# Output projection: the last twelve column tiles computed as six Strassen pairs

## The chip, the cores and the metric

The kernel runs on one core of a Trainium2 chip. Its engines are TensorE (PE in the profile; its weight loads are listed apart as PEld), VectorE (DVE), ScalarE (ACT), GpSimd (POOL) and SyncE (SP, which here only issues DMAs). They run side by side, each through its own list of instructions in a fixed order, and wait for each other through semaphores. The metric is the device time of one execution in microseconds; times below are medians of several executions.

## The reference, cut to what matters

One layer of a decoder: a combined input projection, two token mixers (sparse attention and a gated linear recurrence), a merge, and an output projection with a residual. 512 prompt tokens and 64 sample tokens share the weights, so the kernel treats them as 576 columns. The change touches only the last line:

```
u_att = einsum('btc,cd->btd', o_att * silu(g_att), w_att_out)
u_rnn = einsum('btc,cd->btd', h_rnn * silu(g_rnn), w_rnn_out)
m = sigmoid(gm_att) * u_att + sigmoid(gm_rnn) * u_rnn
return x + einsum('btd,de->bte', m, w_out)        # 576 x 2048 times 2048 x 2048
```

## The kernel before

Everything is kept with channels on the 128 partitions and the 576 tokens along the free dimension, cut into two halves h of 288 columns. A projection's output is cut into tiles of 128 channels. The list `tiles` holds them in order of work: input projection, then `ur` and `ua` (the two branch projections, whose merged result is the activation m, in 16 row blocks of 128 channels), then `y`, the 16 tiles of the output projection. Each `y` tile has two units u: a unit is 8 weight blocks of 128x128, one half of the 2048 rows that are summed.

A **slot** is the work of one unit on one half: 24 matmuls of 288 columns (L1483 to L1485). There are three for each weight block because float32 is kept by splitting both operands into a high part and a rest: high weight times high activation, high times rest, rest times high. A `y` tile has four slots (h0u0, h0u1, h1u0, h1u1), and its two units are added up in one PSUM bank for each half. The banks have tags: `g`, `s` and `t` with two each, `o` and `m` with one.

Weights come in by DMA (`raw`, two buffers). ACT rounds a unit to its high part (`w_high`, tile `whi`, L210), and DVE subtracts to get the rest (`w_low`, tile `wlo`, L216). Both have three buffers in rotation (`WHL = 3`), so the split of a unit waits until the matmuls of the unit three before have read theirs. After a half of a `y` tile is summed, DVE evacuates the bank and adds the residual (L541), and SP stores the tile (L543).

What sets the order: the program is written out slot by slot, and each engine gets its instructions in the order in which the code emits them. In each turn of the slot loop that is: the high parts that are due, then what was booked for this slot with `at(...)`, then the low parts and the next weight loads, the residual loads, then the evacuations (`evac`) of the products that the turn before emitted, then what was booked "behind", and last this slot's own matmuls. So on DVE a turn's low part stands ahead of its evacuations. The unit `(n, u, at)` in `wunits` says in which turn a unit is split.

Of the kernel before, what the change touches and what calls it, by code (L numbers as in the profile page):

```python
# [10 lines left out]
F = mybir.dt.float32  # L11
R = mybir.dt.float32r
# [12 lines left out]
FULL = (0, 1)  # L25
CF, PG = 18, 22
SCH = 22, 38, 66, 5

D = 2048
SEQ = 512  # L30
DB = 8
# [82 lines left out]
def nsa_rglru_step(ctx, tc, a, o):  # L114
# [25 lines left out]

    cst = cp.tile([128, CONST.shape[1]], F, name="cst")
    par = cp.tile([128, NPAR], F, name="par")
    wcs = cp.tile([128, 4, 32], F, name="wcs")
    wcp = cp.tile([128, 32], F, name="wcp")
    pt_sb = cp.tile([1, DB * NPAGE], I32, name="pt_sb")

# [12 lines left out]
    ot_d = {g: dp.tile([128, 2, 512], F, name=f"ot_{g}") for g in range(KG)}  # L159
    kc_d = {b: dp.tile([128, 4, 64], F, name=f"kc_{b}") for b in range(KEPT, DB)}  # L160
    gs_d = dp.tile([48, 64], F, name="gs_d")

# [15 lines left out]
    slots, wunits = [], []  # L178
# [19 lines left out]
    def w_load(k):  # L198
        if k >= len(wunits):
            return  # L200
        n, u, _ = wunits[k]
        t = wp.tile([128, 8, 128], F, tag="raw", name="raw", bufs=WRAW)
        S.dma_start(t, tiles[n][2][u])
        raw[k] = t
# [90 lines left out]
    rstd = cp.tile([128, NT], F, name="rstd")  # L295
    e2 = cp.tile([128, NT], F, name="e2")
    e2t = cp.tile([128, 4], F, name="e2t")
    gq8 = cp.tile([128, 1], F, name="gq8")
# [45 lines left out]
    def etile(name):  # L344
        return ep.tile([128, NT], F, tag="e", name=name, bufs=4)

# [6 lines left out]
    def evac(kind, h, b):  # L353
        hs = slice(h * HF, h * HF + HF)
        z = b[:, :HF]
        name = kind[0]
        if name == "gn":
            if h == 0:
# [166 lines left out]
        elif name == "ua":  # L525
# [7 lines left out]
            A.activation(mh[j][:, hs], m[:, hs], AF.Copy)  # L533
            V.tensor_sub(ml[j][:, hs], m[:, hs], mh[j][:, hs].bitcast(F))
        elif name == "y":
            j = kind[1]
            if h == 0:
                held["y"] = etile("y")
            t = held["y"]
            r = res_in[j]  # L540
            V.scalar_tensor_tensor(t[:, hs], z, 0.25, r[:, hs], OP.mult, OP.add)  # L541
            if h == 1:
                store(lambda: S.dma_start(o["y"][j], t), 1)  # L543
# [778 lines left out]


    psteps, ssteps, pages = prompt_steps(), None, compress()
    prompt_done = False
# [33 lines left out]
    def first_products(s):  # L1359
# [13 lines left out]
        if s == 7:  # L1373
            for h in range(2):
                evs.append((tiles[1][0], h, gbs[h]))

    def sample_work(s):
# [8 lines left out]
    for s, (n, h, u) in enumerate(slots):  # L1386
        now[0] = s
        kind, m, units = tiles[n]
        if s == slot_of[first_r]:
# [7 lines left out]
            att.close()  # L1397
            rp_["h"] = ctx.enter_context(tc.tile_pool(name="hp", bufs=1))
            rp_["s"] = ExitStack()
            rp_["p"] = rp_["s"].enter_context(tc.tile_pool(name="rp", bufs=1))  # L1400
            rnn_begin()
        if s == slot_of[first_u] - 9:
# [3 lines left out]
            rp_["s"].close()  # L1406
            rp_["p"] = ctx.enter_context(tc.tile_pool(name="up", bufs=1))
            for ct in range(8):
                at(s + 3 * ct // 2, lambda ct=ct: oa_make(ct))
        ws = []  # L1410
        while wnext < len(wunits) and wunits[wnext][2] <= s:
# [33 lines left out]
        for n2 in range(n, len(tiles)):  # L1445
# [6 lines left out]
            if name == "y" and j not in res_in:  # L1452
                res_in[j] = rp_["p"].tile([128, NT], F, tag="tgi", name="res", bufs=4)
                S.dma_start(res_in[j], xin[j // 2, :, j % 2, :])
        for e in evs:
# [5 lines left out]
        if n == 1:  # L1461
            first_products(s)
            continue
        wh, wl = whl[n, u]
        last = u == len(units) - 1
        for step, (h2, k) in enumerate([(h, k) for k in range(8)]):
# [12 lines left out]
            elif name == "y":  # L1479
                r_h, r_l = mh[kk], ml[kk]  # L1480
            else:
                r_h, r_l = xh[kk], xl[kk]
# [19 lines left out]
def _layout(x):  # L1502
# [83 lines left out]
```

## Time and profile before

| | us |
|---|---|
| median of 3 runs (1724.31 to 1725.62) | 1725.07 |
| the profiled execution | 1724.24 |
| its span | 1722.5 |
| PE busy / DVE busy / ACT busy | 1691.8 / 1074.8 / 796.8 |
| granted TensorE clock, mean | 0.999 |
| `y` stage, from about | 1515 |
| last matmul starts | 1718.61 |

The page counts an engine's busy time, cuts the span into slices, follows the chain of work that ended last back from the end, and groups instructions by line. The line numbers are those of the kernel before. Matmuls are pipelined: one is listed as 0.29 us long, but the next starts some 0.13 us after it.

### The profile page before, as it was taken

The numbers are of one execution on the slowest core, as the hardware profiler recorded it, in microseconds if no ns is written. First come the engines' busy times: TensorE is split into PE (matmuls) and PEld (weight loads), VectorE is DVE, ScalarE is ACT, GpSimd is POOL, SyncE is SP. The second block draws the span as 40 slices with busy tenths as digits, with TensorE's granted clock in tenths as the row PEclk, the third lists the DMA queues.
The fourth block names the chain that finished last, engine by engine and source line by source line (L and its number), as shares of the span: only waits on it lengthen the run. The fifth ranks groups of instructions, "written<-read, shape, count | busy, mean of one in ns | idle before, by whom it ended". The sixth has DMA issues, their size and how long they took to land. (4 is left out here: it accounts for less than half of the span.)

```text
span 1722.5 us, 33473 instructions
## 1 busy us (share of the span) xinstructions
PE 1691.8 (98%) x12637; PEld 1661.5 (96%) x12637; DVE 1074.8 (62%) x2290; ACT 796.8 (46%) x1487; POOL 476.9 (28%) x503
## 2 busy tenths in 40 slices
PE   9999999999999999999999999999999999999999
PEld 8999989998998999999999999999999999999999
DVE  6578678778867876457777775676664344432221
ACT  6434553553455454367677663666663122211110
POOL 0035334442543344165555540000013111100000
PEclk9999999999999999999999999999999999999999
DMA  6367435434533444367576664222226434333432
GB/s 221 119 208 236 153 105 167 123 111 128 156 117 110 146 143 140 120 183 211 186 215 202 188 187 127 79 92 78 92 95 234 134 115 135 127 127 126 143 115 78
DMA packets 143139, 248.55 MB, mean 144 GB/s; under 512 B 19457, under 2 KB 78466, under 8 KB 142722
## 3 DMA queue, kind: packets, MB, share of 16 engines
q1 hardware_dynamic: 142978, 246.42, 44.5%
q8 instruction: 99, 1.62, 0.4%
q14 instruction: 62, 0.51, 0.1%
HBM read 223.40 MB, written 31.35 MB: 148 GB/s over the span
## 5 line engine op out<-in xcount | busy, mean ns | idle before, releaser
L1483 PE MATMUL g<-xh,whi 128*128 128x288 f32 x2400 | 717.1, 299 | 0.1
L1485 PE MATMUL g<-xh,wlo 128*128 128x288 f32 x2400 | 708.3, 295 | 2.8 <-DVE wlo L216 2.7
L1484 PE MATMUL g<-xl,whi 128*128 128x288 f32 x2400 | 707.4, 295 | 0.0
L1485 PEld LDWEIGHTS g<-xh,wlo 128*128 128x128 f32 x2400 | 450.8, 188 | 3.7 <-DVE wlo L216 3.7
L1483 PEld LDWEIGHTS g<-xh,whi 128*128 128x128 f32 x2400 | 451.4, 188 | 1.6 <-ACT c L388 0.3
L1484 PEld LDWEIGHTS g<-xl,whi 128*128 128x128 f32 x2400 | 451.3, 188 | 1.3
L216 DVE TENSOR_TENSOR wlo<-raw,whi 128x1024 fp32r<-128x1024 f32 x216 | 282.9, 1310 | 105.8 <-ACT whi L210 105.5
L210 ACT ACTIVATE whi<-raw 128x1024 fp32r<-128x1024 f32 x216 | 227.4, 1053 | 214.9 <-PE g L1484 209.8
L835 POOL TENSOR_TENSOR cr<-cr,wcs 128x512 f32<-128x512 f32 x128 | 179.6, 1409 | 143.8 <-DMA cr<-in_cmp 126.2
L1485 PE MATMUL g<-mh,wlo 128*128 128x288 f32 x512 | 150.8, 295 | 0.0
L1484 PE MATMUL g<-ml,whi 128*128 128x288 f32 x512 | 150.8, 294 | 0.0
L687 ACT ACTIVATE p<-p,sm,rq 128x128 f32<-128x128 f32 (+3 forms) x128 | 83.0, 650 | 146.4 <-DVE sm L684 146.4
L1483 PE MATMUL g<-mh,whi 128*128 128x288 f32 x512 | 150.7, 294 | 0.0
L944 POOL TENSOR_TENSOR skl<-kr,skh 128x512 fp32r<-128x512 f32 x80 | 114.2, 1430 | 122.5 <-ACT skh L943 88.1
L695 POOL TENSOR_SCALAR p<-p,sm 128x128 f32<-128x128 f32 (+3 forms) x128 | 70.3, 562 | 220.5 <-DVE sm L692 98.5
L706 DVE TENSOR_TENSOR pt<-t,pt 128x512 fp32r<-128x512 f32 x96 | 66.2, 689 | 64.3 <-ACT pt L705 62.9
L1485 PEld LDWEIGHTS g<-mh,wlo 128*128 128x128 f32 x512 | 96.0, 188 | 0.0
L1483 PEld LDWEIGHTS g<-mh,whi 128*128 128x128 f32 x512 | 96.0, 188 | 0.0
L1484 PEld LDWEIGHTS g<-ml,whi 128*128 128x128 f32 x512 | 96.0, 188 | 0.0
L1046 DVE TENSOR_TENSOR sv<-vr,sv 128x256 fp32r<-128x256 f32 (+1 forms) x120 | 77.4, 672 | 17.5 <-ACT sv L1042 17.3
L841 DVE TENSOR_REDUCE skvx<-cr 128x16 f32<-128x512 f32 x128 | 86.6, 677 | 0.4
L533 ACT ACTIVATE mh<-ur 128x288 fp32r<-128x288 f32 x32 | 14.3, 447 | 145.0 <-POOL ur L529 145.0
(323 smaller groups left out, 2985.8 us busy)
## 6 DMA issues: line engine op xcount, KB each, us to landing
raw<-in_w_in SPq DMA_DIRECT2D x152, 512.0 KB, 3.5
cr<-in_cmp SPq DMA_DIRECT2D x128, 256.0 KB, 3.6
kr<-in_selk SPq DMA_DIRECT2D x128, 128.0 KB, 3.1
vr<-in_selv SPq DMA_DIRECT2D x128, 128.0 KB, 3.1
raw<-in_w_out SPq DMA_DIRECT2D x32, 512.0 KB, 3.3
tg<-gm SPq DMA_DIRECT2D x32, 288.0 KB, 4.4
tgi<-tg SPq DMA_DIRECT2D x32, 288.0 KB, 3.9
raw<-in_w_rnn SPq DMA_DIRECT2D x16, 512.0 KB, 3.5
```

Of the source, the lines that this page charges most:

```text
L210: A.activation(hi, raw[k], AF.Copy)
L216: V.tensor_sub(lo, raw.pop(k), hi.bitcast(F))
L687: A.activation(p[:, :n], p[:, :n], AF.Exp, bias=sm[:, 1, r - r0:r - r0 + 1], scale=rq[:, i, r:r + 1], accum_out=sm[:, 2, r - r0:r - r0 + 1])
L695: G.tensor_scalar(p[:, :n], p[:, :n], sm[:, 3, r - r0:r - r0 + 1], 1.0, op0=OP.mult, op1=OP.mult)
L706: V.tensor_sub(lo, t, hi.bitcast(F))
L835: G.tensor_tensor(v, v, wcs[:, :, None, :].to_broadcast([128, 4, 4, 32]), op=OP.mult)
L841: V.tensor_reduce(x.kvx[:, :, 8 + n * 4:12 + n * 4], v, axis=AX.X, op=OP.add)
L944: G.tensor_tensor(kl, t, kh.bitcast(F), op=OP.subtract)
L1046: V.tensor_sub(v[:, :, :, 1, :], src, v[:, :, :, 0, :].bitcast(F))
L1483: T.matmul(gb[:, :HF], wh[:, k, :], r_h[:, hs], start=kk == 0, stop=False)
L1484: T.matmul(gb[:, :HF], wh[:, k, :], r_l[:, hs], start=False, stop=False)
L1485: T.matmul(gb[:, :HF], wl[:, k, :], r_h[:, hs], start=False, stop=last and k == 7)
```

## The change

The tiles `y` 0 to 3 stay as they were (`YSTD = 4`), but for which row blocks make up a unit: u0 now has the even blocks of m, u1 the odd ones. The tiles 4 to 15 are taken two at a time (j, j+1) as kind `Y`, and a pair is computed with Strassen's scheme in Winograd's form: the output is seen as 2x2 (two channel tiles, two token halves), the sum over rows as two halves (even, odd blocks). Seven products of one slot each take the place of eight. Four sums of weight units (`y_sum`, DVE) and four sums of activations for each pair of row blocks (`y_factors`, DVE) feed them. The activation sums are made once, in the slots of the first four tiles, from float32 rows of m that are stored to HBM when they are made (`m_d`) and read back (`y_fetch`). A product is added from PSUM into one, two or three quarters of the residual tile (`y_evac`), and two pairs of products share a bank: u2 is summed on top of u0, u6 on top of u3. The unit of a product is split three turns ahead of its slot.

Beside this, `e` tiles have five buffers instead of four, some constants move to a pool that is closed early, and the weight rows lie in another order in HBM.

```diff
-    for j in range(16):
+    for j in range(YSTD):
         tiles.append((("y", j), 128, [a["w_out"][j, 0], a["w_out"][j, 1]]))
+    for j in range(YSTD, 16, 2):
+        tiles.append((("Y", j), 128, [None] * 7))
...
+        if kind[0] == "Y":
+            for u in range(7):
+                slots.append((n, 0, u))
+                unit_of[n, u] = len(wunits)
+                wunits.append((n, u, base - 3 + u))
+            continue
...
+            if h == 1:
+                S.dma_start(m_d[j], m)
             A.activation(mh[j][:, hs], m[:, hs], AF.Copy)
             V.tensor_sub(ml[j][:, hs], m[:, hs], mh[j][:, hs].bitcast(F))
...
+    def y_factors(i):
+        e, f = e12.pop(i)
+        lo_, hi_ = slice(0, HF), slice(HF, NT)
+        V.tensor_sub(e[:, lo_], e[:, hi_], e[:, lo_])
+        V.tensor_sub(e[:, hi_], f[:, hi_], e[:, hi_])
+        V.tensor_sub(f[:, hi_], f[:, hi_], e[:, lo_])
+        V.tensor_sub(f[:, lo_], f[:, lo_], f[:, hi_])
+        for t, pool, tag, to in ((e, "h", "hr", t13), (f, "p", "t42", t42)):
...
+            A.activation(hi, t, AF.Copy)
+            V.tensor_sub(lo, t, hi.bitcast(F))
...
+        if which == 1:
+            t = ysum[1] = wp.tile([128, 8, 128], F, tag="raw", name="s1", bufs=WRAW)
+            V.tensor_add(t, a21, yraw[j, 1, 1])
+            units = {0: a11, 2: yraw[j, 0, 1], 5: t, 6: yraw[j, 1, 1]}
+        elif which == 2:
+            t = ysum[2] = wp.tile([128, 8, 128], F, tag="raw", name="s2", bufs=WRAW)
+            V.tensor_sub(t, ysum[1], a11)
+            units = {4: t}
+        elif which == 3:
+            V.tensor_sub(a21, a11, a21)
+            units = {3: a21}
+        else:
+            V.tensor_sub(a11, yraw[j, 0, 1], ysum[2])
+            units = {1: a11}
...
+    def y_plan(n, j):
+        b = slot_of[n]
+        at(b - 7, lambda: y_load(j, 0, 0))
+        at(b - 6, lambda: (y_load(j, 0, 1), y_load(j, 1, 1)))
+        at(b - 6, lambda: y_load(j, 1, 0), True)
+        for which, s in ((1, b - 5), (2, b - 4), (3, b - 3), (4, b - 3)):
+            at(s, lambda which=which: y_sum(n, j, which), True)
...
+    YPROD = ((0, 0, "g", True), (1, 1, "s", True), (1, 0, "g", False), (3, 1, "h", True),
+             (2, 1, "t", True), (3, 0, "s2", True), (2, 0, "h", False))
+    def y_product(n, j, u):
+        rows, half, tag, begins = YPROD[u]
+        if begins:
+            ybank[tag] = bank({"h": "g", "s2": "s"}.get(tag, tag))
+        gb = ybank[tag]
+        wh, wl = whl[n, u]
+        for i in range(8):
...
+            T.matmul(gb[:, :HF], wh[:, i, :], r_h[:, HS[half]], start=begins and i == 0, stop=False, skip_group_check=True)
+            T.matmul(gb[:, :HF], wh[:, i, :], r_l[:, HS[half]], start=False, stop=False, skip_group_check=True)
+            T.matmul(gb[:, :HF], wl[:, i, :], r_h[:, HS[half]], start=False, stop=i == 7, skip_group_check=True)
+        evs.append((("Y", j, u), 0, gb))
+    def y_evac(j, u, z):
+        r = res_in[j].rearrange("p c (h t) -> p (c h) t", h=2)
+        to = {0: r[:, 1:], 1: r[:, 1:2], 2: r[:, 0:1], 3: r[:, 3:], 4: r[:, 1:], 5: r[:, 1::2], 6: r[:, 2:3]}[u]
+        V.scalar_tensor_tensor(to, z[:, None, :].to_broadcast([128, to.shape[1], HF]), 0.25, to, OP.mult, OP.add)
...
+    for i in range(8):
+        at(slot_of[first_y] + 3 * i // 2, lambda i=i: y_fetch(i))
+        at(slot_of[first_y] + 2 + 3 * i // 2, lambda i=i: y_factors(i), True)
```

How the instructions stand now, at three places. First DVE in the `y` stage of the kernel before: low parts of units and evacuations of halves take turns (the name behind the arrow is the bank read or the weights split).

```order
L216 TENSOR_TENSOR wlo_19890<-raw_19777,whi_19889 128x1024 [waits DMAHW5_49,PE_49,Activation_49]
L541 SCALAR_TENSOR_TENSOR y_19862<-g_19864,res_19720 128x288 [waits PE_49]
L216 TENSOR_TENSOR wlo_19946<-raw_19834,whi_19945 128x1024 [waits DMAHW7_49,Activation_49]
L541 SCALAR_TENSOR_TENSOR y_19978<-g_19920,res_19836 128x288 [waits DMAHW6_49,DMAHW0_49,PE_49]
L216 TENSOR_TENSOR wlo_20006<-raw_19893,whi_20005 128x1024 [waits DMAHW1_49,PE_49,Activation_49]
```

DVE in the change, around the first slots of the second pair. `wlo_19990` (just ahead of these rows), `wlo_20024`, `wlo_20054`, `wlo_20083`, `wlo_20117` and `wlo_20154` are the low parts of its u0 to u5; `res_19771` is the residual of the pair before, `res_19993` its own; `g_20091` is the bank of u0 and then u2.

```order
L230 TENSOR_TENSOR wlo_20024<-yr_19860,whi_20023 128x1024 [waits PE_49,Activation_49]
L1426 SCALAR_TENSOR_TENSOR res_19771<-t_19998,res_19771 128x864
L230 TENSOR_TENSOR wlo_20054<-yr_19892,whi_20053 128x1024 [waits PE_49,Activation_49]
L1426 SCALAR_TENSOR_TENSOR res_19771<-s_20028,res_19771 128x2x288 [waits DVE_49]
L230 TENSOR_TENSOR wlo_20083<-yr_19899,whi_20082 128x1024 [waits PE_49,Activation_49]
L1426 SCALAR_TENSOR_TENSOR res_19771<-g_19964,res_19771 128x288
L230 TENSOR_TENSOR wlo_20117<-s2_19962,whi_20116 128x1024 [waits PE_49,Activation_49]
L1426 SCALAR_TENSOR_TENSOR res_19993<-g_20091,res_19993 128x864 [waits DMAHW6_49,DMAHW5_49,DMAHW3_49]
L230 TENSOR_TENSOR wlo_20154<-s1_19931,whi_20153 128x1024 [waits PE_49,Activation_49]
L1426 SCALAR_TENSOR_TENSOR res_19993<-s_20128,res_19993 128x288 [waits DVE_49]
```

The evacuation of u0 (out of `g_20091`) stands behind the low part of u4 (`wlo_20117`), which waits for PE and ACT.

PE in the change at the seam of the same pair's u1 and u2:

```order
L1418 MATMUL s_20128<-ml_19226,whi_20023 128x288
L1419 MATMUL s_20128<-mh_19225,wlo_20024 128x288
L1417 MATMUL g_20091<-mh_17586,whi_20053 128x288 [waits DVE_49,Activation_49]
L1418 MATMUL g_20091<-ml_17587,whi_20053 128x288
L1419 MATMUL g_20091<-mh_17586,wlo_20054 128x288
```

The first matmul of u2 now waits for DVE; before, the seam of a tile's two units had no such wait, since its bank was read only after both.

DVE in the change in the slots of the third and fourth plain tile, where the sums of activations and the first pair's sums of weights stand between the low parts and the evacuations (`ye`, `yo`: the rows read back; `g_19659`: the second half of tile 2):

```order
L230 TENSOR_TENSOR wlo_19685<-raw_19537,whi_19684 128x1024 [waits DMAHW4_49,PE_49,Activation_49]
L1380 TENSOR_TENSOR s1_19688<-yr_19657,ya_19650 128x1024 [waits DMAHW5_49,DMAHW2_49]
L1358 TENSOR_TENSOR ye_19606<-ye_19606 128x288 [waits DMAHW6_49]
L1359 TENSOR_TENSOR ye_19606<-yo_19607,ye_19606 128x288 [waits DMAHW7_49,DVE_49]
L1360 TENSOR_TENSOR yo_19607<-yo_19607,ye_19606 128x288 [waits DVE_49]
L1361 TENSOR_TENSOR yo_19607<-yo_19607 128x288 [waits DVE_49]
L1366 TENSOR_TENSOR tl_19695<-ye_19606,th_19694 128x576 [waits Activation_49]
L1366 TENSOR_TENSOR tl_19699<-yo_19607,th_19698 128x576 [waits Activation_49]
L557 SCALAR_TENSOR_TENSOR res_19449<-g_19659,res_19449 128x288 [waits PE_49]
L1384 TENSOR_TENSOR s2_19727<-s1_19688,yr_19604 128x1024
```

Before, nothing but the low parts and the evacuations stood there.

More of the change, by code (lines that the diff above doesn't have):

```diff
@@ L26 @@
 CF, PG = 18, 22
+YSTD = 4
 SCH = 22, 38, 66, 5
@@ L138, in held_bank @@
         return t
-    cst = cp.tile([128, CONST.shape[1]], F, name="cst")
+    cqs = ExitStack()
+    cq = cqs.enter_context(tc.tile_pool(name="cq", bufs=1))
     par = cp.tile([128, NPAR], F, name="par")
-    wcs = cp.tile([128, 4, 32], F, name="wcs")
-    wcp = cp.tile([128, 32], F, name="wcp")
-    pt_sb = cp.tile([1, DB * NPAGE], I32, name="pt_sb")
+    cst = cq.tile([128, CONST.shape[1]], F, name="cst")
+    wcs = cq.tile([128, 4, 32], F, name="wcs")
+    wcp = cq.tile([128, 32], F, name="wcp")
+    pt_sb = cq.tile([1, DB * NPAGE], I32, name="pt_sb")
     def C(name):
@@ L160, in nsa_rglru_step @@
     kc_d = {b: dp.tile([128, 4, 64], F, name=f"kc_{b}") for b in range(KEPT, DB)}
+    m_d = {k: dp.tile([128, NT], F, name=f"m_{k}") for k in range(16)}
     gs_d = dp.tile([48, 64], F, name="gs_d")
@@ L201, in w_load @@
         n, u, _ = wunits[k]
+        if tiles[n][0][0] == "Y":
+            return
         t = wp.tile([128, 8, 128], F, tag="raw", name="raw", bufs=WRAW)
@@ L295, in nsa_rglru_step @@
     rstd = cp.tile([128, NT], F, name="rstd")
-    e2 = cp.tile([128, NT], F, name="e2")
-    e2t = cp.tile([128, 4], F, name="e2t")
+    e2 = cq.tile([128, NT], F, name="e2")
+    e2t = cq.tile([128, 4], F, name="e2t")
     gq8 = cp.tile([128, 1], F, name="gq8")
@@ L344, in etile @@
     def etile(name):
-        return ep.tile([128, NT], F, tag="e", name=name, bufs=4)
+        return ep.tile([128, NT], F, tag="e", name=name, bufs=5)
     def store(fn, delay=2):
@@ L356, in evac @@
         name = kind[0]
+        if name == "Y":
+            y_evac(kind[1], kind[2], z)
+            return
         if name == "gn":
@@ L1321, in oa_low, with y_fetch @@
         oa[ct] = (hi, lo)
+    t13, t42, yraw, ysum = {}, {}, {}, {}
+    e12 = {}
+    def y_fetch(i):
+        e12[i] = etile("ye"), etile("yo")
+        for e, k in zip(e12[i], (2 * i, 2 * i + 1)):
+            S.dma_start(e, m_d[k])
+    def y_factors(i):
[6 more added lines that the diff above has]
+        for t, pool, tag, to in ((e, "h", "hr", t13), (f, "p", "t42", t42)):
+            hi = rp_[pool].tile([128, NT], R, tag=tag, name="th", bufs=16)
+            lo = rp_[pool].tile([128, NT], R, tag=tag, name="tl", bufs=16)
+            A.activation(hi, t, AF.Copy)
+            V.tensor_sub(lo, t, hi.bitcast(F))
+            to[i] = (hi, lo)
@@ new lines, in y_load, with y_sum @@
+    def y_load(j, c, par_):
+        tag, bufs = ("ya", 2) if c and par_ else ("yr", 3)
+        t = rp_["p"].tile([128, 8, 128], F, tag=tag, name=tag, bufs=bufs)
+        S.dma_start(t, a["w_out"][j + c, par_])
+        yraw[j, c, par_] = t
+    def y_sum(n, j, which):
+        a11, a21 = yraw[j, 0, 0], yraw[j, 1, 0]
+        if which == 1:
[12 more added lines that the diff above has]
+            units = {1: a11}
+        for u, t in units.items():
+            raw[unit_of[n, u]] = t
@@ L1375, in first_products @@
                 evs.append((tiles[1][0], h, gbs[h]))
+    for n, t in enumerate(tiles):
+        if t[0][0] == "Y":
+            y_plan(n, t[0][1])
+    for i in range(8):
+        at(slot_of[first_y] + 3 * i // 2, lambda i=i: y_fetch(i))
+        at(slot_of[first_y] + 2 + 3 * i // 2, lambda i=i: y_factors(i), True)
     def sample_work(s):
@@ L1451, in nsa_rglru_step @@
                 S.dma_start(t, tg_d[int(name == "ur"), j])
-            if name == "y" and j not in res_in:
-                res_in[j] = rp_["p"].tile([128, NT], F, tag="tgi", name="res", bufs=4)
-                S.dma_start(res_in[j], xin[j // 2, :, j % 2, :])
+            if name in ("y", "Y") and j not in res_in and s >= slot_of[first_y]:
+                j -= j % 2
+                res_in[j] = res_in[j + 1] = rp_["p"].tile([128, 2, NT], F, tag="res", name="res", bufs=2)
+                S.dma_start(res_in[j], xin[j // 2])
         for e in evs:
@@ L1462, in nsa_rglru_step @@
             first_products(s)
+            continue
+        if kind[0] == "Y":
+            y_product(n, kind[1], u)
             continue
```

29 lines of the change are left out of this document (20 added, 9 removed).

## The prediction

> **What bounds the kernel now.** I read the page's head first, then the slices, the chain of waits, the windows of the `y` stage, and last the order of time at single handoffs.
>
> ```profile
> span 1722.5 us, 33473 instructions
> PE 1691.8 (98%) x12637; PEld 1661.5 (96%) x12637; DVE 1074.8 (62%) x2290; ACT 796.8 (46%) x1487; POOL 476.9 (28%) x503
> PE 45%; DVE 1%; ACT 0%; issue 0%; DMA 0%; SPq 0%; DVEq 0%; ACTq 0%
> 1550.00:1600.00 50.00, 50.00 (x380) 50.00 (x379) 13.47 (x16) 8.50 (x8) 0.00 (x0) 1.00 0.39 132
> 1600.00:1650.00 50.00, 50.00 (x380) 50.00 (x379) 13.47 (x16) 8.50 (x8) 0.00 (x0) 1.00 0.38 132
> ...
> 1527.15 0.33 SPq L203 DMA_DIRECT2D raw<-in_w_out  x1
> ...
> 1539.87 0.33 SPq L203 DMA_DIRECT2D raw<-in_w_out  x1
> ...
> L1485 PE MATMUL g<-mh,wlo 128*128 128x288 f32 x512 | 150.8, 295 | 0.0
> ```
>
> TensorE is the bound, in the `y` stage without a gap: busy 50.00 of 50.00 us at clock 1.00 while DVE has 13.47 and ACT 8.50, and no idle time ahead of the `y` matmuls (last row). The weight loads of one `y` tile and the next are 12.72 us apart, so a tile of 96 matmuls takes 12.72, a matmul 0.1325 and a slot of 24 takes 3.18. Nothing but fewer or faster matmuls shortens this stage, and every wait of PE lengthens it one for one.
>
> **The gain.** A pair took 2 x 12.72 = 25.44 us and now has seven slots, 22.26. Six pairs: 6 x 3.18 = **-19.1 us** (144 matmuls), if PE never waits.
>
> **The wait inside each pair.** The order of DVE in the change puts the evacuation of u0 behind the low part of u4, and u2 may not write its bank before that evacuation has read it; PE's own row for u2's first matmul shows the wait. That it is this evacuation and not u2's own low part follows from the rows after it: u3 and u4 wait for DVE no more, so the wait of u2 already covers their low parts, which stand before the evacuation. The low part of u4 needs its high part on ACT, and that needs a `whi` buffer: three in rotation, those of u1, u2 and u3 still unread, so it is u1's, free when u1's matmuls end. So u2 waits for a chain that starts only as u1 ends. The handoffs and lengths, in order of time:
>
> ```profile
> 1702.55 0.29 PE L1484 MATMUL g<-ml,whi 128*128 128x288 f32 x1
> ...
> 1702.88 1.06 ACT L210 ACTIVATE whi<-raw 128x1024 fp32r<-128x1024 f32 x1 [8.46 <-PE g L1484]
> ...
> 1703.98 1.23 DVE L216 TENSOR_TENSOR wlo<-raw,whi 128x1024 fp32r<-128x1024 f32 x1 [3.70 <-ACT whi L210]
> ...
> 1502.36 1.23 DVE L216 TENSOR_TENSOR wlo<-raw,whi 128x1024 fp32r<-128x1024 f32 x1 [0.49 <-ACT whi L210]
> 1503.50 0.45 DVE L528 SCALAR_TENSOR_TENSOR tgi<-tgi,g 128x288 f32<-128x288 f32 x1
> ...
> 570.63 1.22 DVE L216 TENSOR_TENSOR wlo<-raw,whi 128x1024 fp32r<-128x1024 f32 x1
> ...
> 571.90 0.40 PE L1485 MATMUL g<-xh,wlo 128*128 128x288 f32 x1 [1.59 <-DVE wlo L216]
> ...
> L541 DVE SCALAR_TENSOR_TENSOR y<-g,res 128x288 f32<-128x288 f32 x32 | 14.6, 458 | 86.7 <-PE g L1485 86.7
> L706 DVE TENSOR_TENSOR pt<-t,pt 128x512 fp32r<-128x512 f32 x96 | 66.2, 689 | 64.3 <-ACT pt L705 62.9
> ```
>
> ACT follows PE's end by 0.04 (1702.55 + 0.29 to 1702.88), DVE follows ACT by 0.04, PE follows DVE by 0.05 (571.85 to 571.90), and a DVE instruction starts 0.09 before the listed end of the one ahead (1503.50 against 1503.59). Count from when u2's first matmul could start. The last reader of u1's high part is its 23rd matmul, which starts 0.265 earlier and ends 0.03 later; ACT 0.07 to 1.13; low part 1.17 to 2.40; evacuation from 2.31. This one adds a bank into three quarters, 864 elements, a size that no row has. From 288 (458 ns) and 512 (689 ns) an element costs 1.03 ns, so 1.05 us by my estimate; bounds are 0.46, if only the 288 columns of the bank counted, and 1.37, three times L541. It ends at 3.36 and PE starts at **3.4** (2.8 to 3.7). Six pairs: **+20.4 us** (16.9 to 22.3). The other shared bank is safe: u6 waits for the evacuation of u3, which follows the same kind of chain from u4's end, 0.07 + 1.06 + 0.04 + 1.23 - 0.09 + 0.46 = 2.8, and u5's 3.18 lie over it.
>
> **The wait at the first pair.** DVE has to make all activation sums, and the first pair's weight sums, during the four plain tiles: 16 slots, 50.9 us.
>
> ```profile
> L534 DVE TENSOR_TENSOR ml<-ur,mh 128x288 fp32r<-128x288 f32 x32 | 14.7, 459 | 45.4 <-ACT mh L533 45.4
> L1295 DVE TENSOR_TENSOR hrl<-rg,hrh 128x576 fp32r<-128x576 f32 x8 | 6.1, 759 | 5.3 <-ACT hrh L1294 5.3
> raw<-in_w_out SPq DMA_DIRECT2D x32, 512.0 KB, 3.3
> 10.00:15.00 5.00, 4.55 (x29) 3.77 (x28) 4.80 (x6) 4.71 (x8) 0.00 (x0) 1.00 1.03 419
> ```
>
> One `y_factors` is four subtractions of 288, each on the result of the one before (0.46 and a handoff of 0.04, so 0.50), and two rests of 576 (0.76), behind ACT: 3.4 us. Eight make 27. Until the fourth weight sum there are also six low parts (1.14 each, 6.8), six evacuations (2.2), four weight sums (4.7) and some six handoffs from ACT of 0.3: 43 us in all. They start when the first half of tile 0 is summed, 6.7 us into the stage, so the fourth sum ends near 49.5, if no transfer is late. Then come the high part of u1 (1.1), its low part (1.2) and only then the evacuation of tile 3's first half (0.5), whose bank the first product takes: 52.3 or later, against 50.9. The stage also moves 16 re-read rows of 288 KB, 10 weight units of 512 KB and two double residuals, some 11 MB; at the 419 GB/s of the last row, where transfers kept all the DMA engines busy, that is 26 us of 51, but one queue issues all of it in order, and the first sum needs the unit that is issued last. If it comes two or three us late, so does all the rest of DVE's list: 3.7 to 4.8 us of wait instead of 1.4. I take **+2.5 us**, between the ends.
>
> **The clock.** Matmuls after a pause may run at half the clock. This trace has two pauses to compare, each given as the stretch of 3.41 us with the pause in it, and what followed the second:
>
> ```profile
> 528.01:531.42 3.41, 1.77 (x12) 1.24 (x11) 2.52 (x4) 2.67 (x4) 3.34 (x4) 1.00 0.04 14
> ...
> 568.96:572.38 3.42, 1.83 (x13) 1.52 (x12) 3.32 (x7) 0.00 (x0) 1.22 (x1) 1.00 0.00 0
> 572.38:575.80 3.42, 3.42 (x17) 3.42 (x16) 1.92 (x6) 1.99 (x3) 0.00 (x0) 0.50 0.79 271
> ...
> 574.09 0.44 PE L1483 MATMUL g<-xh,whi 128*128 128x288 f32 x1
> 574.33 0.44 PE L1484 MATMUL g<-xl,whi 128*128 128x288 f32 x1
> ```
>
> Half an idle stretch is the edge: PE busy 1.77 of 3.41 kept the clock, 1.83 lost it for just one stretch of 3.42 us, in which matmuls start 0.24 us apart instead of 0.1325. My pauses of 3.4 us are as long as a stretch. Wherever the boundary falls, one of the two stretches it cuts keeps at most 1.7 us of PE, mostly far less, so I expect a loss each time. A whole half-clock stretch holds 3.41 / 0.24 = 14.2 matmuls where 25.7 would fit: 1.53 us lost. If it begins inside the pause, on average 0.85 us of it is idle anyway: 1.15. Mean 1.34; six pairs 8.0, and 0.8 for the first pair's shorter pause: **+8.8 us** (0 to 10.5).
>
> The Trainium skill (TensorE: Matmul & The Clock Gate, section "Part 1: The HAM clock gate") says that the gate falls to half after at least one idle window of about 3.4 us, with windows that run freely. By that a pause of 3.4 us almost never fills a whole window, and the clock term is 0. The trace differs: it lost the clock with PE busy 1.83 of 3.42. The rule is the first rival.
>
> **What is hidden.** The 24 weight sums (1.23 like a low part, L216), 18 more splits and wider evacuations bring DVE to 7 x 1.14 + 4 x 1.14 + 4.1 = 16.6 us of a pair's 22.3, ACT to 7.4: neither is a bound, only the order on DVE is. The 16 stores of m, in the `ua` slots on SP's queue, wait for POOL's addition, and the gate and weight loads behind them wait too; those are issued about three slots (9.5 us) ahead and land in under 4, so I give 0; without that cover each would cost its 2 us. The end of the program keeps its shape:
>
> ```profile
> 1718.61 0.29 PE L1485 MATMUL g<-mh,wlo 128*128 128x288 f32 x1
> ...
> 1718.94 0.46 DVE L541 SCALAR_TENSOR_TENSOR y<-g,res 128x288 f32<-128x288 f32 x1 [5.94 <-PE g L1485]
> 1719.42 0.34 SPq L543 DMA_DIRECT2D out_y<-y  x1
> ```
>
> One evacuation of 288 and one store, now of half the size: 0, give or take 0.5.
>
> **The sum**, against the profiled execution of 1724.24 us (span 1722.5 and 1.7 around it): -19.1 + 20.4 + 2.5 + 8.8 = +12.6, 1736.8. The median of the runs shown lies 0.8 above that execution, so 1737.7: I predict **1738 us**.
>
> **Rivals.**
>
> *The clock holds* (0.20). For it: the stretch at 528 us kept its clock with PE busy for 1.77. Against it: the one at 572, and that my pauses are twice as long as these. Then -19.1 + 20.4 + 2.5 = +3.8: 1729.
>
> *The evacuation is not late, and the gain stands* (0.08; this ends faster). If the high part of u4 could take a buffer that u0 freed, its chain would start 3.18 us earlier and leave 0.2 per pair, too short for the clock: -19.1 + 1.4 + 2.5 = -15: 1710. It decides at the point where ACT's split of u4 is released, by u0's end or by u1's. For it: the rows of the order name the engine that is waited for, not the instruction. Against: three buffers and three units unread, and u3 and u4 without a wait of their own.
>
> *The re-read rows starve DVE* (0.08). The re-reads sit on one queue with the weights, each behind the tile buffer it needs, and DVE takes them in order. If the last weight unit comes some 8 us late and not 2 to 3, PE waits twice before the first pair, some 10 us instead of 2.5: 1745. For it: a row that waits blocks everything behind it on SP. Against: 26 us of transfers in 51, and loads that land in 3.3.
>
> **How the numbers follow.** Forecast 0.64, rivals 0.20, 0.08, 0.08. The forecast's own range is 1733 to 1744 (the bounds of the evacuation, of the first wait and of the clock's share). For 8 in 10 I go down to the clock that holds and up to the starved start: **1727 to 1747**. 0.2% (3.45 us) is about what a measurement of this kernel can tell from no change. Slower by more than that: the forecast, the starved start and a little over half of the second case, 0.83; within it: the rest of that case, 0.09; faster: 0.08.
>
> **What would show it.** In the `y` stage PE should have six gaps of 3.4 us ahead of u2's first matmul (L1417), put down to DVE, some 27 us apart, and one of 1 to 5 us at the first product of the first pair. Ahead of each gap's end: ACT, low part, an evacuation of 864 of about 1.05 us, without idle time on DVE between the last two. The clock column should show half in the stretch behind most gaps, with matmuls 0.24 apart. A pair should last 25.7 us, some 27 with the clock. If the six gaps are absent or under 0.5 us, I am wrong on the buffer or the bank; if they are there at full clock, on the clock; if PE waits long before slot 16, on the transfers.

## The result and the profile after

The change made the kernel slower: 1745.47 us (median; 1744.26 to 1746.31) against 1725.34 (1724.31 to 1725.76), a ratio of 1.0117, 95% interval 1.0099 to 1.0135. The forecast was 1738, within 1727 to 1747, slower. The profiled execution has a span of 1742.5 against 1722.5: 20.0 us more.

The head of the page of the changed kernel, PE's waits, and the windows of the `y` stage (PE, its weight loads, DVE, ACT, POOL, each busy time and count; then clock, DMA share and GB/s):

```profile
span 1742.5 us, 33426 instructions
PE 1688.4 (97%) x12493; PEld 1656.8 (95%) x12493; DVE 1164.6 (67%) x2398; ACT 824.6 (47%) x1521; POOL 473.8 (27%) x503
PE g L1417 <- DVE res L1426: 20.0, 6, 3.3
...
PE g L1417 <- DVE res L557: 4.5, 1, 4.5
1500.00:1550.00 50.00, 50.00 (x380) 50.00 (x379) 33.01 (x57) 17.21 (x25) 4.82 (x6) 1.00 0.70 233
1550.00:1600.00 50.00, 40.86 (x280) 40.22 (x279) 31.37 (x41) 13.31 (x15) 0.00 (x0) 0.90 0.36 130
1600.00:1650.00 50.00, 43.33 (x304) 42.92 (x303) 30.40 (x33) 13.79 (x13) 0.00 (x0) 0.93 0.40 132
```

The 144 matmuls are gone (12637 to 12493), but where PE did 380 matmuls in 50 us it now does 304. Six waits of 3.3 us stand at L1417, one of 4.5 at the first pair, and the clock is below 1. One of the six, in order of time, with PE, ACT and DVE from the last matmul of u1 to the restart (columns: start, duration, engine, line, operation; in brackets the idle time ahead and what ended it):

```profile
1663.36 0.29 PE L1419 MATMUL s<-mh,wlo 128*128 128x288 f32 x1
1663.56 1.06 ACT L224 ACTIVATE whi<-s 128x1024 fp32r<-128x1024 f32 x1 [2.07 <-PE s L1418]
...
1664.65 1.22 DVE L230 TENSOR_TENSOR wlo<-s,whi 128x1024 fp32r<-128x1024 f32 x1 [1.54 <-ACT whi L224]
1665.79 1.05 DVE L1426 SCALAR_TENSOR_TENSOR res<-g,res 128x864 f32<-128x864 f32 x1
...
1666.99 0.58 PE L1417 MATMUL g<-mh,whi 128*128 128x288 f32 x1 [3.33 <-DVE res L1426]
...
1667.36 0.44 PE L1418 MATMUL g<-ml,whi 128*128 128x288 f32 x1
```

The chain is the one forecast: u1 ends, ACT makes the high part of u4 in the buffer that u1 held, DVE its low part, then the evacuation of u0 of 864 elements in 1.05 us, and only then u2 starts, with matmuls 0.24 apart, at half clock. The stretches of 3.41 us with that pause in it and behind it:

```profile
1663.36:1666.77 3.41, 0.29 (x3) 0.06 (x1) 2.12 (x2) 1.06 (x1) 0.00 (x0) 1.00 0.93 278
1666.77:1670.18 3.41, 3.19 (x13) 3.23 (x14) 0.07 (x1) 0.00 (x0) 0.00 (x0) 0.50 0.82 278
```

PE was busy 0.29 of 3.41 and lost the clock for the next stretch. All six pauses did so, with 0.69 down to 0.23 us of PE in their stretch. The first pair started later than forecast, as DVE's order shows:

```profile
1525.79 0.46 DVE L557 SCALAR_TENSOR_TENSOR res<-g,res 128x288 f32<-128x288 f32 x1 [4.72 <-DMA res<-in_xT]
...
1557.27 1.23 DVE L1380 TENSOR_TENSOR s<-yr,ya 128x1024 f32<-128x1024 f32 x1 [2.84 <-DMA yr<-in_w_out]
1561.77 0.45 DVE L557 SCALAR_TENSOR_TENSOR res<-g,res 128x288 f32<-128x288 f32 x1
...
1569.30 1.23 DVE L1390 TENSOR_TENSOR yr<-yr,s 128x1024 f32<-128x1024 f32 x1
1571.73 1.22 DVE L230 TENSOR_TENSOR wlo<-yr,whi 128x1024 fp32r<-128x1024 f32 x1 [1.20 <-ACT whi L224]
1572.87 0.45 DVE L557 SCALAR_TENSOR_TENSOR res<-g,res 128x288 f32<-128x288 f32 x1
```

DVE stood idle twice with its list waiting: 4.72 us for the residual of the first tile, 2.84 for the weight unit that is issued last. During the first 1.8 of the 4.72 the half itself was still being summed (its last matmul ends at 1522.84), so the residual cost the other 2.9. The fourth weight sum ended at 1570.5, then came u1's high part (1.2 us of idle DVE), its low part and only then the evacuation for which the first product waited.

### The profile page after: what moved, and what is told of

It reads as the page before. It is cut to its first block, busy times and chain, and to the rows that moved or that the text cites. A ratio compares the mean times of both kernels' runs of the same rounds, so it can differ in the third digit from the quotient of the medians.

```text
span 1742.5 us, 33426 instructions
## 1 busy us (share of the span) xinstructions
PE 1688.4 (97%) x12493; PEld 1656.8 (95%) x12493; DVE 1164.6 (67%) x2398; ACT 824.6 (47%) x1521; POOL 473.8 (27%) x503
## 5 line engine op out<-in xcount | busy, mean ns | idle before, releaser
L230 DVE TENSOR_TENSOR wlo<-raw,whi 128x1024 fp32r<-128x1024 f32 x192 | 256.1, 1334 | 44.5 <-ACT whi L224 44.2
L224 ACT ACTIVATE whi<-raw 128x1024 fp32r<-128x1024 f32 x192 | 201.5, 1050 | 60.8 <-PE g L1612 55.5
L1613 PE MATMUL g<-oah,wlo 128*128 128x288 f32 x256 | 75.5, 295 | 0.0
L1613 PE MATMUL g<-hrh,wlo 128*128 128x288 f32 x256 | 75.4, 295 | 0.0
L1612 PE MATMUL g<-oal,whi 128*128 128x288 f32 x256 | 75.4, 295 | 0.0
L1611 PE MATMUL g<-oah,whi 128*128 128x288 f32 x256 | 75.4, 294 | 0.0
L1612 PE MATMUL g<-hrl,whi 128*128 128x288 f32 x256 | 75.3, 294 | 0.0
L1611 PE MATMUL g<-hrh,whi 128*128 128x288 f32 x256 | 75.3, 294 | 0.0
```

The source lines that it names most:

```text
L224: A.activation(hi, raw[k], AF.Copy)
L230: V.tensor_sub(lo, raw.pop(k), hi.bitcast(F))
L1611: T.matmul(gb[:, :HF], wh[:, k, :], r_h[:, hs], start=kk == 0, stop=False)
L1612: T.matmul(gb[:, :HF], wh[:, k, :], r_l[:, hs], start=False, stop=False)
L1613: T.matmul(gb[:, :HF], wl[:, k, :], r_h[:, hs], start=False, stop=last and k == 7)
```

## The experiments

All ratios are to the kernel before, timed beside the run in question.

| run | median us | ratio, 95% interval |
|---|---|---|
| the change | 1745.47 | 1.0117 (1.0099-1.0135) |
| e1 u2 in a bank of its own | 1713.95 | 0.9925 (0.9909-0.9942) |
| e2 pairs' evacuations first | 1717.40 | 0.9949 (0.9932-0.9965) |
| e3 pauses filled, 24 matmuls | 1735.33 | 1.0058 (1.0041-1.0075) |
| e4 no pairs, preparing kept | 1725.13 | 0.9995 (0.9986-1.0005) |
| e5 splits one slot later | 1714.48 | 0.9933 (0.9917-0.9950) |
| e6 e2, factors on GpSimd | 1712.43 | 0.9926 (0.9910-0.9941) |
| e7 e6, start moved forward | 1712.07 | 0.9924 (0.9909-0.9938) |
| e8 12 matmuls in the pause | 1735.69 | 1.0060 (1.0040-1.0079) |
| e9 6 matmuls in the pause | 1743.68 | 1.0103 (1.0081-1.0124) |
| e10 e2, start moved forward | 1708.55 | 0.9896 (0.9878-0.9913) |
| e11 e10, u2 in its own bank | 1706.10 | 0.9881 (0.9864-0.9899) |
| e12 e10's start, e9's pauses | 1734.10 | 1.0048 (1.0028-1.0067) |

**What makes u2 wait: e1, e2, e5.** Theory: the evacuation of u0's bank, late because a low part that waits for u1's buffer stands ahead of it. Each run takes away one link: the shared bank, the place behind the low part, or the wait of that low part for u1.

```diff
-(1, 0, "g", False)        # e1: YPROD of u2
+(1, 0, "o", True)
```

> u2 gets a bank of its own instead of the three quarters of u0's bank; nothing else changes. Theory (u2 waits for the evacuation of u0's bank, which stands on VectorE behind the low part of u4, and each such wait costs the clock of the next stretch of 3.41 us): all six gaps of 3.3 us ahead of L1417 go, with the six half-clock stretches behind them: 1745.5 - 20.0 - 8.4 = 1717, within 3; the 4.5 and 1.3 us ahead of the first pair stay. Rival A (VectorE has too much to do in a pair in bulk): PE waits for VectorE at other places of the pair, 1735 or more. Rival B (the clock is lost for another reason than the gaps, so it stays lost without them): 1745.5 - 20.0 = 1725.5 with half-clock stretches left.

Here the quarter that takes u0's and u2's product lacks u0's; the work on PE is the same.

```diff
+        for e in [e for e in evs if e[0][0] == "Y"]:     # e2: ahead of w_low(k)
+            evac(*e)
+        evs = [e for e in evs if e[0][0] != "Y"]
         for k in ws:
             w_low(k)
```

> u2 keeps u0's bank, but the evacuations of a pair are put ahead of the low part of the same turn on VectorE. Theory (it is the order on VectorE that makes the evacuation late): u0's evacuation ends about 1.1 us after u0's last matmul, inside u1's 3.18 us: the six gaps and their half-clock stretches go, 1717 within 3, as with a bank of its own. Now the low part stands behind an evacuation, but its unit is needed two slots later. Rival (the evacuation isn't held by the low part of u4 but by something that both orders have, the sums or the products' end): gaps stay at 3.3 us and the time at 1745.

```diff
-                wunits.append((n, u, base - 3 + u))      # e5
+                wunits.append((n, u, base - 2 + u))
```

> The split of each weight unit of the y stage is done one slot later in the program's order, so that on ScalarE and VectorE the evacuation of u0 stands ahead of the split that takes u1's buffer. Theory (u0's evacuation is late because it stands behind a split that waits for u1's buffer): it now stands behind the split that takes the buffer that u0 frees, whose chain begins 3.18 us earlier; gaps of 0.2 us are left and the clock is kept: 1745.5 - 19 - 8.4 = 1718, within 3. If the split is now late for its own product (its unit is needed one slot earlier after it than before), PE would wait at other products of each pair, seen ahead of L1417 to L1419 behind the low part: 0.5 to 1 us each. Rival (the bank is late for a reason other than u1's buffer): 1745, gaps as before.

In e5 the fourth weight sum overwrites the weights of u0 ahead of their split, so the first product uses other numbers; the instructions are the same.

All three fell to 1714 to 1717, where 1717 to 1718 was expected. e5 came out 3.5 us lower than expected; in its trace the first pair waits 1.60 us and not 4.53. That e1 came out 3.0 lower isn't explained by its trace. In e1 PE is busy for 50.00 of 50.00 us inside the pairs. In e2 one pause of 0.57 us and five of 0.2 are left, in e5 six of 0.15. The chain in e2 and the same place in e5:

```profile
1603.66 1.23 DVE L230 TENSOR_TENSOR wlo<-yr,whi 128x1024 fp32r<-128x1024 f32 x1 [1.32 <-ACT whi L224]
1604.80 1.05 DVE L1426 SCALAR_TENSOR_TENSOR res<-g,res 128x864 f32<-128x864 f32 x1
...
1606.00 0.37 PE L1417 MATMUL g<-mh,whi 128*128 128x288 f32 x1 [0.20 <-DVE res L1426]
```

```profile
1644.57 1.06 ACT L224 ACTIVATE whi<-yr 128x1024 fp32r<-128x1024 f32 x1 [2.05 <-PE g L1418]
1645.66 1.23 DVE L230 TENSOR_TENSOR wlo<-yr,whi 128x1024 fp32r<-128x1024 f32 x1 [0.72 <-ACT whi L224]
1646.81 1.05 DVE L1426 SCALAR_TENSOR_TENSOR res<-g,res 128x864 f32<-128x864 f32 x1
```

In e2 a low part still ends right ahead of the evacuation: it is that of the turn before, which waited for u0's buffer. So in both runs the chain starts 3.18 us earlier, at u0's end, and the evacuation ends within 0.2 us of u1's end. e1 shows that the bank is the link on PE's side, e2 the order on DVE, e5 the buffer that the split waits for. DVE's load in bulk (rival A) is excluded: nothing else in the pairs waits in e1, where DVE is busy 38.46 of 50. Rival B (half-clock stretches without pauses) is excluded too: of e1's stretches inside the pairs, the two at the start of the first pair (1575.63 to 1582.46, behind a wait of 3.01) were at half, and none after them.

**What the clock costs: e3, e8, e9.** The pauses stay, and part of each is filled with matmuls into a bank that nobody reads.

```diff
+        if u == 2:
+            idle = bank("o")
+            for i in range(24):                          # e8: 12, e9: 6
+                T.matmul(idle[:, :HF], wh[:, i % 8, :], mh[2 * (i % 8) + 1][:, HS[0]], start=True, stop=True)
```

> The gaps stay, but 24 matmuls into a bank that nobody reads are put ahead of u2's product in each pair (the work of the output is the same, 144 matmuls are added), so that PE is busy for 24 x 0.1325 = 3.18 us of a gap of 3.33. Theory (the half-clock stretches come from the pauses): clock stays at 1.0 through the six pairs, u2 starts some 3.4 us after u1's end as before or at most 0.3 later, 1745.5 - 8.4 = 1737, within 3. Rival (the loss of clock is not tied to PE's pauses, or costs no time): 1745.5.

> As e3 with 12 unused matmuls in place of 24 (1.59 us), so that each pair keeps a pause of 3.33 - 1.59 = 1.74 us. Theory (a stretch of 3.41 us loses the clock of the next when PE is busy for about half of it or less): a pause of 1.74 seldom empties half a stretch, so at most two of the six pairs lose the clock, 1735 to 1738, and the start of u2 comes where it did. Rival A (any pause of over a microsecond loses the clock): six half-clock stretches, 1745. Rival B (only a wholly idle stretch loses it): none, 1735, but that would leave unexplained the six of the changed kernel, whose pauses are 3.33.

> As e3 with 6 unused matmuls (0.8 us), so that each pair keeps a pause of 3.33 - 0.8 = 2.5 us; in e8 a pause of 1.67 kept the clock each time, in the changed kernel one of 3.33 lost it each time. Theory (the next stretch goes to half when PE is busy for about half of a stretch of 3.41 us or less, and its phase against the pause decides): a pause of 2.5 covers more than half of one stretch in about half of the phases, so 2 to 5 of six pairs lose the clock: 1738 to 1743. Rival A (the edge is the length of the pause, at or above 3 us): none lost, 1735. Rival B (any pause over 2 us): six lost, 1745.

With the pauses filled (e3) or halved (e8, six of 1.67 us) the clock stayed at 1.00 behind all six pauses, and the time fell to 1735 to 1736. The excess over the kernel before went from 20.1 to 9.3 and 9.5 us, 10.7 to 10.9 less, by medians that leave some 3 us open. The traces are closer: from the restart behind the first pause to its last matmul the change takes 153.37 us (1585.46 to 1738.83) and e8 144.60 (1586.24 to 1730.84). Of these 8.8 us, 0.4 is not the clock, since a pause with its 12 matmuls is 0.08 shorter than one of 3.33. The six lost stretches cost about 8.4. The half-clock stretches at the first pair are no part of this: e8 has two there like the change, e3 one. e9 missed: its pauses of 2.45 us lost the clock six times out of six, not two to five, and the time stayed near that of the change, as its rival B (any pause over 2 us loses) had it; the first pause of e12, below, excludes that rival. (The unused matmuls never bring u2 forward, since the evacuation sets its start; what they can change is the clock.) The stretches with and behind a pause in e8, and then in e9:

```profile
1661.41:1664.83 3.42, 1.75 (x14) 1.52 (x13) 2.03 (x2) 0.00 (x0) 0.00 (x0) 1.00 0.96 383
1664.83:1668.24 3.41, 3.41 (x28) 3.41 (x28) 0.32 (x1) 1.06 (x1) 0.00 (x0) 1.00 0.58 183
```

```profile
1663.83:1667.25 3.42, 0.97 (x9) 0.74 (x7) 2.19 (x2) 1.06 (x1) 0.00 (x0) 1.00 0.92 335
1667.25:1670.66 3.41, 3.41 (x14) 3.41 (x15) 0.00 (x0) 0.00 (x0) 0.00 (x0) 0.50 0.78 248
```

PE busy 1.75 of 3.42 kept the clock, 0.97 lost it. Neither stretch is wholly idle. The Trainium skill (TensorE: Matmul & The Clock Gate, section "Part 1: The HAM clock gate") has the clock fall after at least one idle window of about 3.4 us; e9 speaks against that, and the length of the stretch, 3.413 us, agrees with it.

**Why all six, and not half of them: e12.** My reading of e9 was that the first loss sets the phase of the next pause against the stretches. e12 starts the pairs at full clock, so the first pause falls anywhere.

```diff
-        for e in [e for e in evs if e[0][0] in ("y", "Y")]:   # against e10
+        for e in [e for e in evs if e[0][0] == "y"]:
...
+            for i in range(6):
+                T.matmul(idle[:, :HF], wh[:, i % 8, :], mh[2 * (i % 8) + 1][:, HS[0]], start=True, stop=True)
```

> e10's clean start (no half-clock stretch at the first pair), but with the pairs' evacuations behind the low parts again and 6 unused matmuls, so that each pair keeps a pause of 2.45 us as in e9, where all six lost the clock. Theory (the loss sets the phase: while the clock holds, a pair takes 22.26 + 0.80 + 2.5 = 25.5 us, which moves the pause by 25.5 - 7 x 3.413 = 1.6 us against the stretches, so it falls well inside one by the second or third pair; from the first loss on, pairs lengthen to 8 stretches, 27.31, and every later pause loses too): the pairs ahead of the first loss, none to two of them, keep the clock, all after it lose it and their distance goes to 27.2 to 27.31: 1708.5 - 1.2 + 6 x 3.3 + 4 to 6 x 1.5 = 1733 to 1736. Rival (each pause loses by itself, by its own phase or length): losses and kept stretches alternate, distances of 25.5 and 27 mixed, or all six lost from the first on in a row with no approach to 27.31.

The six restarts, and the stretches around the first two:

```profile
1577.17 0.40 PE L1427 MATMUL g<-mh,whi 128*128 128x288 f32 x1 [2.45 <-DVE res L1436]
...
1602.91 0.40 PE L1427 MATMUL g<-mh,whi 128*128 128x288 f32 x1 [2.45 <-DVE res L1436]
...
1630.22 0.40 PE L1427 MATMUL g<-mh,whi 128*128 128x288 f32 x1 [2.45 <-DVE res L1436]
...
1657.50 0.40 PE L1427 MATMUL g<-mh,whi 128*128 128x288 f32 x1 [2.45 <-DVE res L1436]
...
1684.80 0.40 PE L1427 MATMUL g<-mh,whi 128*128 128x288 f32 x1 [2.45 <-DVE res L1436]
...
1712.10 0.40 PE L1427 MATMUL g<-mh,whi 128*128 128x288 f32 x1 [2.45 <-DVE res L1436]
```

```profile
1572.69:1576.11 3.42, 2.03 (x16) 1.79 (x14) 1.51 (x3) 1.06 (x1) 0.00 (x0) 1.00 0.91 279
1576.11:1579.52 3.41, 2.35 (x18) 2.35 (x19) 1.01 (x2) 0.00 (x0) 0.00 (x0) 1.00 0.59 238
1600.00:1603.41 3.41, 0.96 (x7) 0.72 (x6) 2.19 (x2) 0.63 (x1) 0.00 (x0) 1.00 0.99 364
1603.41:1606.83 3.42, 3.42 (x17) 3.42 (x16) 0.00 (x0) 0.00 (x0) 0.00 (x0) 0.50 0.73 260
```

The first pause lay across a boundary, left 2.03 and 2.35 us of work in the two stretches, and kept the clock. The next restart came 25.74 us later, 1.85 more than seven stretches, and that pause fell inside one stretch and lost it. From there on the restarts are 27.28 to 27.31 us apart, eight stretches (27.31), and each pause loses again. A loss costs 27.3 - 25.74 = 1.56 us, the whole-stretch value of the forecast (1.53), not its mean of 1.34. So a pair that loses a whole stretch puts the next pause at nearly the same place in its stretch, and that one loses as well. e9 does the same, with restarts 27.24 to 27.30 apart.

In the change the distances also grow: 27.09, 27.19, 27.25, 27.26 and 27.28 us. Its first restart lies 0.61 us behind the start of the half-clock stretch (1585.46 against 1584.85), its last 0.15 (1721.53 against 1721.38), so more and more of that stretch is work and the loss grows towards a whole one. Whether any periodic pause would be drawn to a whole number of stretches isn't shown: 25.74 + 1.53 = 27.27 lies within 0.04 us of eight stretches by itself, and no run has a pair of another length.

**What preparing costs: e4.**

```diff
-YSTD = 4
+YSTD = 16
```

> No pair at all: all sixteen tiles of the output projection are plain, as before the change, but the stores of m, the sixteen re-reads, and the sums and splits of activations (y_factors) stay, with nobody reading them; the weight sums are gone. It measures the cost of preparing alone. Theory (preparing costs little: some 1.1 us that PE lost before the y stage and 1.3 to 2.1 us for the second plain tile, whose bank waits for the late residual): 1726 + 3 = 1729, within 2. Rival (the extra transfers starve the loads of weights or the residual, so PE waits again and again): 1733 or more, with PE waiting for low parts in the y stage.

Nothing: 1725.13 against 1726.24, and PE busy 55.00 of the first 55 us of the stage, with the stores, the re-reads and all factors in place. My 3 us were wrong. Two thirds of that I had read from the 1.27 us wait at 1562 in the changed kernel, and put down to the residual; it goes away with the weight units and their sums, one of which stands ahead of that evacuation in DVE's list. The late residual alone isn't enough: DVE waits for it in e4 too, for 4.43 us, and PE doesn't. The 1.15 us that the changed kernel's profile lost ahead of the stage (PE reaches its 11000th matmul at 1502.85, before at 1501.70) aren't the change either: e4 has the same program up to there and is at its 11000th at 1500.96. The changed kernel's profile has four half-clock stretches ahead of the stage where before's has one.

**The first pair: e6, e7, e10.** Theory: DVE's list is late by its idle times and by its order.

```diff
-        V.tensor_sub(e[:, lo_], e[:, hi_], e[:, lo_])         # e6: all four
+        G.tensor_tensor(e[:, lo_], e[:, hi_], e[:, lo_], op=OP.subtract)
```

> The evacuations of pairs ahead of the low parts, as in e2, and the four subtractions of each y_factors on GpSimd (idle in this stage) in place of VectorE, their rests on VectorE one slot later. Theory (the 4.5 us ahead of the first pair are VectorE's list, which stands late behind a residual of the first tile and a weight unit that is issued last): 8 x 1.84 = 14.7 us leave that list, so the first pair waits for at most 1.5 us and loses at most one stretch of clock: 1717.4 - 3 to 4.5 - 1.5 to 2.9 = 1711, within 2. Rival (GpSimd's subtractions of 288 take so much longer than 0.8 us, or slow VectorE's, that the last factors are late): the first wait stays at 4 us or grows, 1717 or more.

```diff
+            S.dma_start(res_in[0], xin[0])                    # e7: ahead of the first re-reads
+                at(b - 9, lambda c=c, par_=par_: y_load(j, c, par_))   # first pair; was b - 7, b - 6
-        for e in [e for e in evs if e[0][0] == "Y"]:
+        for e in [e for e in evs if e[0][0] in ("y", "Y")]:
```

> As e6, and also: the residual of the first two tiles is issued ahead of the first re-reads, the four weight loads of the first pair two to three slots earlier, and the plain tiles' evacuations too stand ahead of the low part of their turn. Theory: the wait of about 2 us at the second plain tile shrinks to 1 or less and the first pair starts without a wait, so that 1.6 us of pauses of 0.3 inside pairs and the 1.1 us from before the stage are what is left beside the gain: 1726 - 19.1 + 1.6 + 1.1 = 1709.6, within 2. Rival (the earlier loads only push the re-reads back, and the factors are late instead): as e6 or slower.

e10 is e7 with the four subtractions on VectorE again.

> As e7, but with the subtractions of y_factors back on VectorE: e2 with the first residual ahead of the re-reads, the first pair's weight loads at slot 7 in place of 9 and 10, and evacuations of plain tiles ahead of the low part too. In e7 the subtractions on GpSimd took up to 1.67 us each in place of 0.81, and VectorE's work beside them 1.83 in place of 1.22. Theory (the first pair waits in e2 because VectorE stood idle 3.25 us for the weight unit that is issued last and 5.14 for the residual, and because the evacuation stands behind u1's low part, 2.4): without these the list ends before its product is due, PE waits at most 0.5 us there and keeps its clock: 1726 - 19.1 + 1.5 = 1708.5, within 2. Rival (VectorE's list of 43 us is itself too long for the start): a wait of 2 us or more at the first pair stays, 1712 or more.

e6 gained 5.0 us on e2, but kept a wait of 2.5 at the first pair (at most 1.5 expected). e7 brought nothing more: its first product waited 3.05 us, and it missed its 1709.6. The reason is in its order of DVE and POOL, and in the window of those 10 us:

```profile
1557.82 1.82 DVE L1383 TENSOR_TENSOR s<-yr,ya 128x1024 f32<-128x1024 f32 x1
...
1558.64 1.68 POOL L1360 TENSOR_TENSOR yo<-yo 128x288 f32<-128x288 f32 x1
...
1556.00:1566.00 10.00, 9.47 (x71) 9.23 (x70) 9.81 (x9) 3.31 (x5) 9.61 (x7) 1.00 0.28 96
```

DVE is busy for 9.81 of the 10 us and GpSimd for 9.61, with nine and seven operations. A weight sum that takes 1.22 alone takes 1.82, a subtraction of 0.81 alone takes 1.68. The Trainium skill (SBUF — State Buffer, section "SBUF: two separate sides") says that VectorE with two SBUF inputs and GpSimd share a pair of ports which one holds for a whole instruction; these rows agree with waiting for each other.

With the subtractions back on VectorE (e10) the forecast of 1708.5 came to 1708.55. DVE's wait for the residual is 3.17 us in place of 5.14 in e2, that for the weight unit is gone, and the first product follows the fourth sum directly:

```profile
1566.01 1.23 DVE L1390 TENSOR_TENSOR yr<-yr,s 128x1024 f32<-128x1024 f32 x1
1567.15 0.45 DVE L557 SCALAR_TENSOR_TENSOR res<-g,res 128x288 f32<-128x288 f32 x1
...
1567.74 0.37 PE L1423 MATMUL g<-mh,whi 128*128 128x288 f32 x1 [1.10 <-DVE res L557]
```

The wait of 1.10 is more than the 0.5 expected. Whether the list itself is too long, as the rival has it, isn't shown by this, since DVE still stood idle for the residual. No half-clock stretch is left in the stage, except the last, after the end of the work.

**A version that beats both: e11.** u2 gets its own bank, and u0's product goes to all four quarters.

```diff
-(1, 0, "g", False)                                           # against e10: YPROD of u2
+(1, 0, "o", True)
-        to = {0: r[:, 1:], 1: r[:, 1:2],
+        to = {0: r, 1: r[:, 1:2],
```

> As e10, and u2 has its own bank, so that u0's product is added to all four quarters (1152 elements) and u2's to one. Theory: the last six pauses of 0.2 us go as well: 1.2 below e10, 1707.3; nothing else waits for the longer evacuation of u0 (by 0.3 us a pair on VectorE). Rival: the longer evacuation delays the low part behind it and a product waits: as e10 or slower.

1706.10 us, 2.4 below e10 where 1.2 were expected (their intervals overlap). PE in the pairs, as before the change:

```profile
1600.00:1650.00 50.00, 50.00 (x380) 50.00 (x379) 39.14 (x41) 16.78 (x16) 0.00 (x0) 1.00 0.45 146
1650.00:1700.00 50.00, 50.00 (x380) 50.00 (x379) 35.81 (x38) 14.86 (x14) 0.00 (x0) 1.00 0.22 78
```

It is 1.2% below the kernel before (0.9881) and 39 us below the change. A fourth buffer for the split weights, which would free the split of u4 from u1 directly, wasn't tried.

## Why the prediction was right or wrong

The sum of the spans: 20.0 us were found where the working gave 12.6.

- **The gain, -19.1: right.** e11, with one wait of 1.2 us left, is 19.5 us below the kernel before, by medians that leave some 3 us open.
- **The wait in each pair, +20.4: right in chain, place and size.** Pauses of 3.33 us, and 0.23 more from one restart to the next (in e8 a pair without loss takes 25.75 us: 22.26 of products, 1.59 of unused matmuls, a pause of 1.67, and 0.23): 6 x 3.56 = 21.4. The 864-element evacuation took 1.05, as estimated. Of the rivals, *the evacuation is not late* fell by the profile itself, and e5 shows what it would have been worth.
- **The first pair, +2.5: wrong in size.** The pauses were 4.53 and, ahead of it, 1.27, with the restarts 6.3. The step that failed is the allowance for "if no transfer is late". Without lateness the sum gave 1.4, with the fourth weight sum 49.5 us into the stage; it ended at 54.2 (1570.53, from 1516.36), 4.7 later, and 1.4 + 4.7 is the wait that was found. I allowed the weight unit two or three us (with 1.4 that is 3.4 to 4.4, not 3.7 to 4.8) and took 2.5. The unit was 2.84 late, and the residual of the first tile, which I did not look at, kept DVE 2.9 us longer at the head of its list. The late list also delayed an evacuation of the last plain tile but one, a second wait that I had not foreseen. e10 moved both transfers and the evacuation, and 1.1 us are left; it does not tell their shares apart. The rival of starved re-reads had two waits, but neither its size (5.8 us of pauses against some 10, a unit 2.84 us late against 8) nor its cause is borne out: e4 carries the same re-reads, and the residual's wait, without any wait of PE.
- **The clock, +8.8: right in direction, too small.** The six pairs cost 8.4 where 8.0 was forecast. Each half-clock stretch began inside the pause, as the working allowed for, but only 0.61 to 0.15 us of it was idle, not 0.85 on average. The larger miss is the first pair, some 2.0 in place of 0.8: its pause of 4.53 us left PE busy for 1.15 of 3.41 us in one stretch and 1.14 in the next, and both lost the clock (half from 1571.20 to 1578.03, with work from 1573.47). The two together make 10.4. The rival *the clock holds* fell: each of the six pauses lost the clock, and in e9 none of the stretches that lost it was wholly idle. "Half an idle stretch is the edge" was about right, but its two rows (1.77 kept, 1.83 lost) can't show an edge, since the one with more work is the one that lost.
- **Hidden work, 0, and the tail, 0: right.** For the first, e4 has the preparing without a wait, and in e1 PE is never idle inside the pairs with all their weight sums; the last matmul to the end of the span is 3.7 us, before 3.9.

-19.1 + 21.4 + 6.3 + 10.4 - 0.2, and 1.15 lost ahead of the stage, which belongs to that execution and not to the change, make 19.95. The forecast of 1738 was 7.5 us short, mostly by the first pair (3.8), the clock (1.6) and the waits (1.0). The forecast's own range, 1733 to 1744, did not hold the result of 1745.47: the start lay above its bound of 4.8 and the clock at its bound of 10.5. The wide range held it only because it reached up to the starved start, a rival that did not come true; that part is luck.

## What to carry to other kernels

A bank that is shared by two products puts the evacuation of the first on the path of the second: look up what stands ahead of that evacuation in its engine's list, and what that waits for; moving three lines was worth 28 us here. A pause of PE cost more than its length here once it took more than about half of a clock stretch, and a periodic one that had lost the clock lost it every time after, since a pair with its loss came within 0.2 us of eight stretches; pauses of half the length (1.67 us) cost the pause alone, six times of six. When work is moved onto an engine with a fixed list, read the first item of that list too: a transfer that is late there makes everything behind it late.

## What the runs showed of the hardware that was not expected

- After the first lost clock the restarts are close to eight stretches of 3.413 us apart (27.09 to 27.31 us) whether the pause is 3.33 us (the change) or 2.45 with 0.8 of other work (e9, e12), where without a loss they are 25.74. Taking 0.9 us off the pause saved no clock, taking 1.7 off saved all of it.
- The edge is a band. In the fourteen profiles, of the stretches at full clock ahead of the last matmul, all 27 with PE busy for less than 1.5 us lost the clock of the next, none with more than 1.85 did, and between these 25 lost it and 18 kept it. Four of e8's stretches (1.75 us) lie in this band and kept it. A stretch that was itself at half clock took more busy time: 2.79 us lost the next one too (e1, 1575.63 to 1579.05), 2.81 kept it (the change, 1584.85 to 1588.27).
- VectorE and GpSimd slowed each other by up to a half and up to a factor of two (1.22 to 1.82, 0.81 to 1.68 us) in subtractions and sums of two SBUF operands.
- The same residual load took 2.04 us to be issued on SyncE in the change, where it is the fourth of a row of DMAs, and 0.37 in e10, where it is the second and the re-read that is now the fourth took 1.88:

```profile
1519.74 2.04 SPq L1579 DMA_DIRECT2D res<-in_xT  x1
```

```profile
1518.07 0.37 SPq L1542 DMA_DIRECT2D res<-in_xT  x1
...
1518.99 1.88 SPq L1352 DMA_DIRECT2D yo<-m  x1
```

In these two it went by the place in the row and not by the transfer. But in e2 the sixth of the row was the slow one, with 1.15, so what sets it stays open.
